# Written order on TensorE, hand-placed transposes of the norms, and raw weight sums by DMA, in a two-layer hybrid trunk

## The chip, the cores and the metric

The kernel runs on one core of a Trainium2 chip. The metric is device time in microseconds. Before the change three runs took 1724.76 us in the median (1724.73 to 1726.11). Engines: TensorE (PE in the profile, PEld its weight loads), VectorE (DVE), ScalarE (ACT), GpSimd (POOL) and SyncE (SP). SP issues plain loads, POOL issues the DMAs that add into what they write.

## What is computed

Two layers over 512 tokens of width 1024, all in float32:

```
x = x + 0.5 * SwiGLU_1(RMSNorm(x))          # width 2816
h = RMSNorm(x);  z = h @ W_in               # q, k, v, conv_B, conv_C, conv_h
x = x + concat([sliding-window attention, B * conv3(C * h_conv)]) @ W_out
x = x + 0.5 * SwiGLU_2(RMSNorm(x))
```

and a final RMSNorm. SwiGLU is `(silu(h @ w_gate) * (h @ w_up)) @ w_down`.

## The kernel before

**Products.** Every float32 operand is split in a high part (rounded to the format that TensorE takes, a ScalarE cast, L204) and a low part (the difference, a VectorE subtraction, L205): `hi`/`lo` for activations, `wh`/`wl` for weights. A product is three matmuls: high by high, low by high, high by low (`stream`, L781). Weights come in raw tiles of 128x1024 (tag `raw`, eight buffers); `wh` and `wl` have three buffers each, and `take_split` asks for a split two groups ahead of its use.

**Seven products for eight.** Most products are grouped in sevens (a Winograd form of Strassen's scheme). The weights' forms are a11, a12, s2, s3, s1, a22, s4, each in two halves h. Raw s1 and s3 are made on the way in: a load, and a second load that POOL's DMA adds to it (L199). Two more sums are made from raw tiles: a11 becomes s2 by adding s1 (L231), and a12 becomes s4 by adding a11 (L256 as a DMA, or L258 on VectorE), according to `how`. The activations' forms are b11, b21, t2, t3, t1, t4, b22 (`Seven.make`, L567 on); t2, for instance, is two VectorE sums (L578, L580), a cast and a subtraction. A form named in `far` is split otherwise (`split_far`, L207): ScalarE writes the negated source into the low part (L209), casts the high part (L210), and a POOL DMA adds the source to the low part (L211).

**Stages.** A SwiGLU is a list of stages: `w` takes two column blocks of gate and up at once (`winograd2`), with seven steps named by `CHAINS`: step 0 accumulates x from b11, step 1 w from b21, step 2 x again from t2, step 3 y from t3, then t1, t4, b22. Each step is 24 wide matmuls, two halves h by two token tiles u by six. `s` is the product with w_down shared in the same manner (`share`; x_s, y_s, w_s in the profile), `d` a plain down product (`down`, L309). The first SwiGLU has its own list (`FIRST`); the three others (`INNER`, `LAST`) begin with `w` on block 0 right after a norm. `mix` does the combined projection, attention and convolution, and multiplies by W_out with `share` in an early order of its own (x_m, y_m, w_m, z_m; `CHAINS_EARLY`), so that the first half of the tokens ends before the second. There t4 is the operand of step 4 (y_m), and t1, t4 and b22 are `far`.

**Norms.** A `Norm` is called with each finished tile of x. It adds the tile's squares (ScalarE). When the four pieces of a half of the tokens are there, `stage` (L522) computes the factor and, for each width half o and token tile t, scales (VectorE, `xn`, L546) and transposes (`turn`: four 128x128 transposes, L551, and copies, L554 to L557). For a norm ahead of a SwiGLU it then makes b11, b21 (after the first half) and t2 (after the second). The transposes take PSUM banks by tag: `aux`, `aux`, `sc`, `sc`, then `mm`, `mm`, `sc`, `sc` (ahead of a SwiGLU). The accumulators x take `mm` too, of which there are four.

**What sets the order.** Each engine issues in an order fixed when the program is made. The start is written by hand; all else is ordered by a scheduler that goes by the order of the code where it can, and on each engine takes a later instruction first when it expects the earlier one's inputs or buffers to be late. So PE's order before the change is nearly the written one, apart from transposes and a few products that were put back. In attention (`attend`) each step writes the product with the values, then the transposes of the probabilities (`Unit.turn`, L1285), then the next unit's scores (L1248, L1249).

Of the kernel before, what the change touches and what calls it, by code (L numbers as in the profile page):

```python
# [13 lines left out]
ALU = mybir.AluOpType  # L14

P = 128
# [56 lines left out]
def trunk_kernel(  # L73
# [53 lines left out]
    def small(name, n=NT, dt=F32):  # L127
        return work.tile([P, n], dt, tag="small", bufs=16, name=name)
# [84 lines left out]
    def need_split(g):  # L213
        while state["split"] <= min(g, len(order) - 1):
            n = state["split"]
            u, what = order[n]
            far = what == "far"
            if what in (None, "wide", "far"):
                need_raw(u if far else u + LOAD_AHEAD)
                raw = raw_of.pop(u)  # L220
            elif isinstance(what, tuple):

                what, h, how = what
                far = how == "far"
                last = {"a11": 0, "a12": 4, "s2": 2, "s3": 6, "s1": 2, "a22": 8, "s4": 4}[what]
                need_raw(u + h if far else u + max(last, 4) + h + LOAD_AHEAD)
                a11, s1, a12, s3, a22 = (raw_of.get(u + 2 * i + h) for i in range(5))
                if what == "s2":
                    late = state["late"] if h else None
                    with tc.issue_after(late) if late else nullcontext():  # L230
                        nc.vector.tensor_add(a11, a11, s1)  # L231
                raw = {"a11": a11, "a12": a12, "s2": a11, "s3": s3, "s1": s1, "a22": a22, "s4": a12}[what]
            else:

                need_raw(u + 4 + LOAD_AHEAD)
                a11, a12, s1, s3, a22 = (raw_of.get(u + i) for i in range(5))
                if what == "s2":
                    nc.vector.tensor_add(a11, a11, s1)
                if what == "s4":
                    nc.vector.tensor_add(a11, a11, a12)  # L240
                raw = {"a11": a11, "a12": a12, "s2": a11, "s3": s3, "s1": s1, "a22": a22, "s4": a11}[what]
                if what == FORMS[-1]:
                    for i in range(5):
                        del raw_of[u + i]
            shape = list(raw.shape)
            hi = wpool.tile(shape, F32R, tag="wh", bufs=3, name=f"wh_{n}")
            lo = wpool.tile(shape, F32R, tag="wl", bufs=3, name=f"wl_{n}")
            if far:
                sent = split_far(hi, lo, raw)
            else:  # L250
                split(hi, lo, raw)
            if isinstance(order[n][1], tuple):
                early = how == "early"
                if what == "s2" if early else what == "s3":
                    if how:
                        nc.gpsimd.dma_start(out=a12, in_=a11, accum_op=ALU.add)  # L256
                    else:
                        nc.vector.tensor_add(a12, a12, a11)  # L258
                done = {
                    "s2": (0,) if early else (),  # L260
                    "s3": (3,) if early else (0, 3),
                    "s1": (1,),
                    "a22": (4,),
                    "s4": (2,),
                }.get(what, ())
                for i in done:
                    del raw_of[u + 2 * i + h]
            split_of[n] = (hi, lo)
            state["split"] += 1
            if far:  # L270

                with tc.issue_after(sent.ins):
                    need_raw(u + LOAD_AHEAD + (4 + h if isinstance(order[n][1], tuple) else 0))
# [23 lines left out]
                nc.tensor.matmul(acc, lo[:, k, :], rhs[k][0], start=False, stop=k == last)  # L297
        return acc

    def down(acts, blocks):  # L300

        last = len(blocks) - 1

        def products(acc, t, i, wh, wl):
            tok = slice(t * P, (t + 1) * P)
            ah, al = acts[blocks[i]]
            for k in range(2):
                for n, (a, w) in enumerate(((ah, wh), (al, wh), (ah, wl))):
                    nc.tensor.matmul(  # L309
                        acc,  # L310
                        a[:, k, tok],
                        w[:, k, :],
                        start=i + k + n == 0,
                        stop=i == last and k == 1 and n == 2,
                    )

        for o in range(2):
            accs = [psum("mm", [P, S], f"down_{state['group']}_{t}") for t in range(NT)]
            if o and last:
                held = [take_split(SPLIT_AHEAD - i)[1:] for i in range(last + 1)]  # L320
                ahead = state["group"]
                for t in range(2):
                    for i, w in enumerate(held):
                        products(accs[t], t, i, *w)
                    yield t, o, accs[t]
                for i, w in enumerate(held):
                    for t in range(2, NT):
                        products(accs[t], t, i, *w)
                        if i == last:
                            yield t, o, accs[t]  # L330
                    need_split(ahead + i)
                continue
            for i in range(last + 1):
                _, wh, wl = take_split()
                for t in range(NT):
                    products(accs[t], t, i, wh, wl)
                    if i == last:
                        yield t, o, accs[t]

    def plan():  # L340
# [25 lines left out]
        def ffn(wg, wu, wd, stages):  # L366
            for what, b in stages:
# [3 lines left out]
                    up(wg, wu, b)  # L371
                if what == "w":
                    seven(
                        lambda o, j, h: ((wg, wu)[o], KC // 2 * j + 2 * h, 2, 2 * b * P, S), None
                    )
                if what == "s":
                    seven(
# [28 lines left out]
    def xt(t, o):  # L406
        return stream_of[2 * o + t // 2][:, t % 2, :]
# [60 lines left out]
    class Norm:  # L468
# [53 lines left out]
        def stage(self, half):  # L522

            i = self.i
            if half == 0:
                self.rooms()
            v, r, y = (small(f"{n}_{i}_{half}", 2) for n in "vry")
            at = 2 * half
            nc.vector.tensor_add(v, self.ss[:, at : at + 2], self.ss[:, NT + at : NT + at + 2])
# [1 line left out]
            nc.vector.tensor_scalar(v, v, 1.0 / D, EPS, op0=ALU.mult, op1=ALU.add)  # L531
            newton(y, r, v)
            for o in range(2):
                for t in (at, at + 1):
                    self.turn(t, o, y[:, t - at : t - at + 1])
                if half == 0 and not self.mixing:
                    self.make(("b11", "b21")[o])
            if half and not self.mixing:
                self.make("t2")

        def turn(self, t, o, by):

            name = f"{self.i}_{t}_{o}"
            tok = slice(t * P, (t + 1) * P)
            xn = g2(f"xn_{name}")
            nc.vector.scalar_tensor_tensor(  # L546
                xn, xt(t, o), by, self.gain[o], op0=ALU.mult, op1=ALU.mult
            )
            tp = psum(self.tags.pop(0), [P, KC // 2, P], f"xt_{name}")
            for j in range(KC // 2):  # L550
                nc.tensor.transpose(tp[:, j, :], xn[:, j * P : (j + 1) * P], ident)  # L551
# [220 lines left out]
                bias[:, h, :], df, -(2.0 ** -(h + 1)), m0, op0=ALU.mult, op1=ALU.add  # L772
            )

    def stream(accs, wh, wl, xh, xl, h, start):

        for u in range(2):
            tok = slice(u * P, (u + 1) * P)
            for k in range(2):
                for i, (x_, w) in enumerate(((xh, wh), (xl, wh), (xh, wl))):  # L780
# [5 lines left out]
                        stop=h + k == 2 and i == 2,  # L786
                        skip_group_check=not start,
                    )

    def share(ops, by, between=None, soon=None, after=None):  # L790

# [3 lines left out]
        for step, (acc, operand, start) in enumerate(chains):  # L795
# [4 lines left out]
                accs[acc] = [psum(tag, [P, S], f"{acc}_{ops.name}_{m}") for m in range(2)]  # L800
            for h in range(2):
                _, wh, wl = take_split()
                stream(accs[acc], wh, wl, xh, xl, h, start)
                if soon:
                    ops.make(*soon.get((step, h), ()))
                if h == 0:
# [18 lines left out]
    def ffn(norm, stages, whole, after=None, late=None):  # L825
# [100 lines left out]
        def winograd2(b, between=None):  # L926


            name = f"{whole}_{b}"
            accs = {}  # L930
            gates = [g2(f"gate_{name}_{t}") for t in range(NT)]
            ups = [None] * NT
            kept = {}
# [5 lines left out]
            for step, (acc, operand, start) in enumerate(CHAINS):  # L939
# [4 lines left out]
                    accs[acc] = [psum(tag, [P, S], f"{acc}_{name}_{u}") for u in range(2)]  # L944
                for h in range(2):
                    _, wh, wl = take_split()
                    stream(accs[acc], wh, wl, xh, xl, h, start)
                    for u in range(2):
                        out = accs[acc][u]
                        if h == 0:  # L950
# [18 lines left out]
                            nc.scalar.activation(gates[2 + u], out, AF.Silu)  # L969
                            nc.vector.tensor_mul(ups[2 + u], ups[2 + u], gates[2 + u])  # L970
                turns(step)
                if not first and step < 4:
                    norm.make(("t3", "t1", "t4", "b22")[step])
                if between:
                    between(step)
            if b in blocks:
# [38 lines left out]
        for i, (what, b) in enumerate(stages):  # L1015
# [25 lines left out]
            if final and not after:  # L1041
# [1 line left out]
                    [(acts[k][0][:, j, :], acts[k][1][:, j, :]) for k in b for j in range(2)]  # L1043
                )
                return
            for n, (t, o, acc) in enumerate(down(acts, b)):
                if b == (0,):
                    norm.make(*{0: ("t3",), 4: ("t1",)}.get(n, ()))
                nc.vector.scalar_tensor_tensor(
# [127 lines left out]
    def mix(l, norm, after):  # L1177
        q = [None] * NH

        mixed = [g8(f"m_{l}_{j}", F32, (P, KC // 2, S)) for j in range(2)]  # L1180
        ops = Seven(mixed, room_g8, f"m_{l}", far=("t1", "t4", "b22"))

        first = state["group"]
        held = [take_split(SPLIT_AHEAD - j) for j in range(3)]
# [1 line left out]
        for t in range(2):  # L1186
            tok = slice(t * H, (t + 1) * H)
            for j, (_, hi, lo) in enumerate(held):
                for k in range(KC):
                    xh, xl = (z[:, tok] for z in norm.h[k])  # L1190
                    for i, (w, x_) in enumerate(((hi, xh), (hi, xl), (lo, xh))):
# [5 lines left out]
                            stop=k == KC - 1 and i == 2,  # L1197
                            skip_group_check=True,
                        )
                if t:  # L1200
                    need_split(first + j + 3)

# [182 lines left out]
        late = ("sc", "sc", "aux", "aux") if mixing else ("mm", "mm", "sc", "sc")  # L1385
        return Norm(i, gain, mixing, ("aux", "aux", "sc", "sc") + late)

    for l in range(DEPTH):
        n1, n2 = stages_of(3 * l + 1), stages_of(3 * l + 2)
        n3 = stages_of(3 * l + 3) if l + 1 < DEPTH else None  # L1390
        ffn(norm, INNER if l else FIRST, 2 * l, n1, None if l else make_bias)
        mix(l, n1, n2)
        ffn(n2, INNER if n3 else LAST, 2 * l + 1, n3)
        norm = n3


# [28 lines left out]
```

## Time and profile before

| | us |
|---|---|
| median of three runs (lowest, highest) | 1724.76 (1724.73, 1726.11) |
| the profiled execution's own time | 1727.49 |
| its span, first to last instruction | 1725.7 |
| PE busy | 1685.2 (98%) |
| DVE busy | 1345.7 (78%) |
| ACT busy | 959.5 (56%) |
| POOL busy | 191.8 (11%) |
| mean granted TensorE clock | 0.992 |

Lines of a view are quoted as they stand. In a timeline a row is start, duration, engine, line, operation, output<-inputs by the program's names without numbers, shapes, and how many instructions were merged; in brackets the idle time before it and who ended it. A row of waits is who waited for whom, total, times and longest. A row of the table of stretches is the stretch, its length, and busy time with instructions of each engine, the granted clock, the DMA engines' busy share and GB/s. A row of a group ends with its total busy time and the mean ns of one, then the idle time before. Durations of matmuls overlap, since they are pipelined; what one costs is the distance from start to start.

### The profile page before, as it was taken

What the parts mean: (1) busy time and instruction counts of PE and PEld (TensorE: products, weight loads), DVE (VectorE), ACT (ScalarE), POOL (GpSimd) and SP (SyncE); (2) the same over time, 40 slices, a digit from 0 to 9 for tenths busy, and PEclk for the clock granted to TensorE, in tenths of its full rate; (3) what the DMA queues carried; (4) which work ended last, traced back from release to release, by engine and by line L of the source; (5) the groups of instructions that cost most, each with busy time, mean ns of one, the idle gap of its engine ahead of it and who ended that gap; (6) DMA issues with size and microseconds to landing.
All of it is one profiled execution on the core that took longest, in us unless ns stands there. A gap on an engine that the chain in (4) does not pass through costs nothing.

```text
span 1725.7 us, 21836 instructions
## 1 busy us (share of the span) xinstructions
PE 1685.2 (98%) x8150; PEld 1405.2 (81%) x8150; DVE 1345.7 (78%) x1762; ACT 959.5 (56%) x1369; POOL 191.8 (11%) x172
## 2 busy tenths in 40 slices
PE   9999999999988999999999999999999799999998
PEld 7888898898867888887778888878888678888877
DVE  7986689868779777799597776995578797776994
ACT  6545555556565555564455555644565655556553
POOL 0011111000210111011101111110002101111101
PEclk9999999999999999999999999999999989999999
DMA  8467788622694767678547776783127947767781
GB/s 244 103 180 194 183 205 210 166 66 62 153 225 123 207 172 189 179 191 222 147 122 196 186 180 184 191 219 112 39 74 166 212 133 191 188 171 190 189 207 49
DMA packets 188206, 285.62 MB, mean 166 GB/s; under 512 B 9124, under 2 KB 72132, under 8 KB 188100
## 3 DMA queue, kind: packets, MB, share of 16 engines
q1 hardware_dynamic: 146340, 204.91, 37.6%
q0 software_dynamic: 41056, 78.65, 26.9%
q8 instruction: 64, 1.05, 0.2%
q10 hardware_dynamic: 704, 0.66, 0.1%
q14 instruction: 42, 0.34, 0.1%
HBM read 268.46 MB, written 2.10 MB: 157 GB/s over the span
## 4 chain that ended last, share of the span: by engine, by line
PE 59%; DVE 6%; issue 2%; ACT 1%; DMA 1%; POOL 0%; ACTq 0%; POOLq 0%; DVEq 0%
PE x L781 18%; PE y L781 9%; PE x_s L781 6%; PE w L781 4%; PE y_s L781 4%; PE down L309 3%; PE x L896 2%; PE acc L291 2%; PE acc L292 2%; PE acc L294 2%; PE at L982 2%; DVE wl L205 1%; PE y L896 1%; DVE raw L231 1%; PE acc L1192 1%
## 5 line engine op out<-in xcount | busy, mean ns | idle before, releaser
L204 ACT CAST wh<-raw 128x1024 fp32r<-128x1024 f32 (+1 forms) x503 | 524.4, 1045 | 557.4 <-PE x L781 137.6
L205 DVE TENSOR_TENSOR wl<-raw,wh 128x1024 fp32r<-128x1024 f32 (+1 forms) x503 | 606.6, 1213 | 269.1 <-ACT wh L204 267.5
L781 PE MATMUL x<-wh,ft 128*128 128x512 f32 x608 | 189.6, 392 | 1.0 <-DVE ft L205 1.0
L781 PE MATMUL x<-wh,fb 128*128 128x512 f32 x608 | 188.5, 390 | 0.0
L781 PE MATMUL y<-wh,ft 128*128 128x512 f32 x608 | 188.5, 391 | 0.0
L781 PEld LDWEIGHTS x<-wh,ft 128*128 128x128 f32 x608 | 113.1, 188 | 25.1 <-DVE ft L205 2.2
L781 PEld LDWEIGHTS x<-wh,fb 128*128 128x128 f32 x608 | 114.3, 188 | 23.4
L781 PEld LDWEIGHTS y<-wh,ft 128*128 128x128 f32 x608 | 113.1, 188 | 22.7
L781 PE MATMUL x<-wl,fb 128*128 128x512 f32 x304 | 118.6, 390 | 0.0
L781 PE MATMUL x<-wl,ft 128*128 128x512 f32 x304 | 118.4, 390 | 0.0
L781 PE MATMUL y<-wl,ft 128*128 128x512 f32 x304 | 118.3, 389 | 0.0
L199 POOL DMA_DIRECT2D raw<-in_ffn_wu_dram x42 | 51.1, 1217 | 585.6 <-DMA raw<-in_ffn_wu_dram 405.2
L781 PE MATMUL w<-wh,fb 128*128 128x512 f32 x304 | 98.6, 409 | 5.3 <-ACT wh L204 5.3
L291 PE MATMUL acc<-hh,wh 128*128 128x512 f32 x240 | 94.6, 394 | 0.0
L294 PE MATMUL acc<-hh,wl 128*128 128x512 f32 x240 | 93.9, 391 | 0.0
L292 PE MATMUL acc<-hl,wh 128*128 128x512 f32 x240 | 93.6, 390 | 0.0
L309 PE MATMUL down<-wh,a 128*128 128x512 f32 x288 | 90.0, 392 | 0.0
L781 PE MATMUL y_s<-wh,ft_s 128*128 128x512 f32 x256 | 80.5, 392 | 5.4 <-ACT wh L204 5.4
L781 PE MATMUL x_s<-wh,ft_s 128*128 128x512 f32 x256 | 78.1, 393 | 1.2 <-ACT wh L204 1.0
L199 POOL DMA_DIRECT2D raw<-in_ffn_wg_dram x42 | 50.9, 1219 | 244.6 <-DVE wl L205 92.3
L781 PE MATMUL x_s<-wh,fb_s 128*128 128x512 f32 x240 | 74.0, 389 | 0.0
L781 PEld LDWEIGHTS w<-wh,fb 128*128 128x128 f32 x304 | 57.4, 195 | 19.6 <-ACT wh L204 8.2
(313 smaller groups left out, 3451.3 us busy)
## 6 DMA issues: line engine op xcount, KB each, us to landing
raw<-in_ffn_wu_dram SPq DMA_DIRECT2D x129, 512.0 KB, 3.7
raw<-in_ffn_wd_dram SPq DMA_DIRECT2D x104, 512.0 KB, 5.4
raw<-in_ffn_wg_dram SPq DMA_DIRECT2D x86, 512.0 KB, 5.0
raw<-in_ffn_wu_dram POOLq DMA_DIRECT2D x42, 512.0 KB, 7.7
raw<-in_ffn_wg_dram POOLq DMA_DIRECT2D x42, 512.0 KB, 6.3
raw<-in_w_in_dram SPq DMA_DIRECT2D x36, 512.0 KB, 3.8
raw<-in_ffn_wd_dram POOLq DMA_DIRECT2D x32, 512.0 KB, 7.8
raw<-raw POOLq DMA_DIRECT2D x20, 512.0 KB, 6.4
```

What stands on the lines that cost most here:

```text
L199: nc.gpsimd.dma_start(out=r, in_=rows_of(*more), accum_op=ALU.add)
L204: nc.scalar.copy(hi, raw)
L205: eng.tensor_sub(lo, raw, f32(hi))
L231: nc.vector.tensor_add(a11, a11, s1)
L291: nc.tensor.matmul(acc, hi[:, k, :], rhs[k][0], start=k == first, stop=False)
L292: nc.tensor.matmul(acc, hi[:, k, :], rhs[k][1], start=False, stop=False)
L294: nc.tensor.matmul(acc, lo[:, k, :], rhs[k][0], start=False, stop=k == last)
L309: nc.tensor.matmul(acc, a[:, k, tok], w[:, k, :], start=i + k + n == 0, stop=i == last and k == 1 and n == 2,)
L781: nc.tensor.matmul(accs[u], x_[:, 2 * h + k, tok], w[:, k, :], start=start and h + k + i == 0, stop=h + k == 2 and i == 2, skip_group_chec ...
L896: nc.tensor.matmul(out, w[:, k, cols], x_[:, k, :], start=start and k + i == 0, stop=k == KC // 2 - 1 and i == 2, skip_group_check=not start,)
L982: nc.tensor.transpose(tp[:, t * P : (t + 1) * P], ups[t][:, c * P : (c + 1) * P], ident)
L1192: nc.tensor.matmul(opened[j][:, tok], w[:, k, :], x_, start=t + k + i == 0, stop=k == KC - 1 and i == 2, skip_group_check=True,)
```

## The change

1. The whole loop over the layers runs under a manual schedule for PE: TensorE issues its instructions in written order. The other engines are ordered as before.
2. `Norm.stage` only scales; it puts the scaled tiles on a list, two at a time. `pull` takes one entry off, transposes it, and makes the forms that follow. `pull` is called at places written by hand: after the last product of token tiles 2 and 3 in `down` (L309); within the last step of `share` where a norm follows; within step 1 of the first `winograd2` pair after a norm; and twice in the opening groups of `mix` (L1192).
3. In the first pair after a norm t3 is made after step 1, t1 and t4 after step 2, b22 after step 3: one step later than before for t3, t1; t2 with the last pull.
4. The first pair of each `INNER` or `LAST` list has `how` = "light": a11 becomes s2 by a DMA on POOL that adds s1, written behind a11's split, and a12 becomes s4 by a DMA too. Two L231 adds and two L258 adds of each of the three pairs leave VectorE, and four 512 KB DMAs come for them.
5. In `mix`, t4 is no longer in `far`: its low part is a VectorE subtraction.

```diff
-                if what == "s2":
+                if what == "s2" and how != "light":
                     late = state["late"] if h else None
                     with tc.issue_after(late) if late else nullcontext():
                         nc.vector.tensor_add(a11, a11, s1)
...
+                if what == "a11" and how == "light":
+                    nc.gpsimd.dma_start(out=a11, in_=s1, accum_op=ALU.add)
                 if what == "s2" if early else what == "s3":
                     if how:
                         nc.gpsimd.dma_start(out=a12, in_=a11, accum_op=ALU.add)
...
                         if i == last:
                             yield t, o, accs[t]
+                            if norm:
+                                norm.pull()
...
-                        lambda o, j, h: ((wg, wu)[o], KC // 2 * j + 2 * h, 2, 2 * b * P, S), None
+                        lambda o, j, h: ((wg, wu)[o], KC // 2 * j + 2 * h, 2, 2 * b * P, S),
+                        "light" if b == 0 else None,
...
             for o in range(2):
+                xns = []
                 for t in (at, at + 1):
-                    self.turn(t, o, y[:, t - at : t - at + 1])
-                if half == 0 and not self.mixing:
-                    self.make(("b11", "b21")[o])
-            if half and not self.mixing:
+                    xns.append(g2(f"xn_{i}_{t}_{o}"))
+                    nc.vector.scalar_tensor_tensor(
+                        xns[-1],
+                        xt(t, o),
+                        y[:, t - at : t - at + 1],
+                        self.gain[o],
+                        op0=ALU.mult,
+                        op1=ALU.mult,
+                    )
+                self.waiting.append((half, o, xns))
+
+        def pull(self):
+
+            if not self.waiting:
+                return
+            half, o, xns = self.waiting.pop(0)
+            for t, xn in enumerate(xns):
+                self.turn(2 * half + t, o, xn)
+            if self.mixing:
+                return
+            if half == 0:
+                self.make(("b11", "b21")[o])
+            elif o:
                 self.make("t2")
...
     def stream(accs, wh, wl, xh, xl, h, start, norm=None):
...
+            if norm:
+                norm.pull()
...
-                stream(accs[acc], wh, wl, xh, xl, h, start)
+                stream(accs[acc], wh, wl, xh, xl, h, start, after if step == 6 else None)
...
-                    stream(accs[acc], wh, wl, xh, xl, h, start)
+                    stream(accs[acc], wh, wl, xh, xl, h, start, norm if fresh and step == 1 else None)
...
-                if not first and step < 4:
-                    norm.make(("t3", "t1", "t4", "b22")[step])
+                if fresh:
+                    norm.make(*{1: ("t3",), 2: ("t1", "t4"), 3: ("b22",)}.get(step, ()))
...
-            for n, (t, o, acc) in enumerate(down(acts, b)):
+            for n, (t, o, acc) in enumerate(down(acts, b, after if final else None)):
...
-        ops = Seven(mixed, room_g8, f"m_{l}", far=("t1", "t4", "b22"))
+        ops = Seven(mixed, room_g8, f"m_{l}", far=("t1", "b22"))
...
+                    if t == 0 and (j, k) in ((1, KC - 1), (2, KC // 2 - 1)):
+                        norm.pull()
...
-    for l in range(DEPTH):
+    with tc.manual_schedule(engines={pe}):
+        for l in range(DEPTH):
```

More of the change, by code (lines that the diff above doesn't have):

```diff
@@ L298, in group, with down @@
         return acc
-    def down(acts, blocks):
+    def down(acts, blocks, norm=None):
         last = len(blocks) - 1
@@ L526, in stage @@
                 self.rooms()
+                self.waiting = []
             v, r, y = (small(f"{n}_{i}_{half}", 2) for n in "vry")
@@ L533, in stage, with turn @@
             for o in range(2):
+                xns = []
                 for t in (at, at + 1):
-                    self.turn(t, o, y[:, t - at : t - at + 1])
-                if half == 0 and not self.mixing:
-                    self.make(("b11", "b21")[o])
-            if half and not self.mixing:
+                    xns.append(g2(f"xn_{i}_{t}_{o}"))
[19 more added lines that the diff above has]
+            elif o:
                 self.make("t2")
-        def turn(self, t, o, by):
+        def turn(self, t, o, xn):
             name = f"{self.i}_{t}_{o}"
             tok = slice(t * P, (t + 1) * P)
[L545 to L548, printed above, removed]
             tp = psum(self.tags.pop(0), [P, KC // 2, P], f"xt_{name}")
@@ L773, in make_bias, with stream @@
             )
-    def stream(accs, wh, wl, xh, xl, h, start):
+    def stream(accs, wh, wl, xh, xl, h, start, norm=None):
         for u in range(2):
@@ L930, in winograd2 @@
             accs = {}
+            fresh = b == 0
             gates = [g2(f"gate_{name}_{t}") for t in range(NT)]
@@ L1386, in stages_of @@
         return Norm(i, gain, mixing, ("aux", "aux", "sc", "sc") + late)
-    for l in range(DEPTH):
[L1389 to L1394, printed above, removed]
+    with tc.manual_schedule(engines={pe}):
+        for l in range(DEPTH):
+            n1, n2 = stages_of(3 * l + 1), stages_of(3 * l + 2)
+            n3 = stages_of(3 * l + 3) if l + 1 < DEPTH else None
+            ffn(norm, INNER if l else FIRST, 2 * l, n1, None if l else make_bias)
+            mix(l, n1, n2)
+            ffn(n2, INNER if n3 else LAST, 2 * l + 1, n3)
+            norm = n3
 _INS = [
```

## The prediction

> **What bounds the kernel now.** I read the page first, for the engine that has least room:
>
> ```profile
> PE 1685.2 (98%) x8150; PEld 1405.2 (81%) x8150; DVE 1345.7 (78%) x1762; ACT 959.5 (56%) x1369; POOL 191.8 (11%) x172
> ```
>
> TensorE (PE) is the bound nearly everywhere, so a change can win only what PE waits, or runs slowly, now. The waits of PE say for whom, in total, times and longest:
>
> ```profile
> PE y_m L781 <- DMA ft_m<-sums_m: 9.5, 2, 4.9
> PE w L781 <- DVE wl L205: 7.2, 4, 2.7
> PE y_s L781 <- ACT wh L204: 5.4, 6, 0.9
> PE w L781 <- ACT wh L204: 5.3, 6, 0.9
> PE x_m L781 <- DVE wl L205: 1.7, 2, 0.9
> ```
>
> Three places: y_m in the output product of each mixing layer; w, the second product of the first gate/up pair after a norm; and y_s in the shared down products. A table of stretches shows what they cost, the granted clock (PEclk) included. First two rows: the y_m wait of layer 0; third: norm to third product, layer 0; fourth: steady state; the 862 rows: the norm between the layers; the last three: layer 1's y_m and norm.
>
> ```profile
> core 0: us, PE busy (x) PEld busy (x) DVE busy (x) ACT busy (x) POOL busy (x), PEclk, DMA share, GB/s
> 491.60:496.40 4.80, 0.25 (x2) 0.00 (x0) 3.39 (x4) 0.93 (x1) 0.00 (x0) 0.86 1.04 294
> 496.40:502.00 5.60, 5.53 (x13) 4.38 (x14) 0.00 (x0) 0.85 (x1) 2.42 (x2) 0.51 0.74 234
> 518.40:538.70 20.30, 15.87 (x67) 11.89 (x67) 19.41 (x27) 8.47 (x15) 0.00 (x0) 0.92 0.17 30
> 560.00:720.00 160.00, 160.00 (x739) 132.79 (x738) 111.43 (x113) 88.34 (x113) 19.44 (x16) 1.00 0.74 187
> 862.50:870.00 7.50, 4.77 (x17) 2.73 (x17) 7.50 (x13) 2.77 (x7) 0.00 (x0) 1.00 0.00 0
> 870.00:874.00 4.00, 4.00 (x16) 3.26 (x17) 3.69 (x5) 1.18 (x2) 0.00 (x0) 0.57 0.00 0
> 862.50:881.50 19.00, 16.15 (x66) 11.83 (x66) 17.96 (x24) 7.82 (x14) 0.00 (x0) 0.91 0.05 10
> 1350.00:1355.00 5.00, 0.13 (x1) 0.00 (x0) 3.27 (x4) 0.92 (x1) 0.00 (x0) 1.00 1.04 298
> 1355.00:1359.00 4.00, 3.96 (x10) 3.12 (x11) 0.00 (x0) 0.00 (x0) 0.88 (x1) 0.57 0.71 271
> 1376.00:1397.70 21.70, 17.91 (x67) 13.52 (x67) 19.61 (x26) 8.02 (x15) 0.00 (x0) 0.76 0.19 35
> ```
>
> In steady state PE never idles and DVE has 30% to spare (111 of 160). After a norm DVE is the full one (19.41 of 20.30), and PE waits for its low parts (wl). After the long y_m waits the clock is at about half.
>
> For unit costs I take two pieces of PE's time, 24 wide products in 5.44 us and four transposes between two products (874.08 to 874.75, less one product):
>
> ```profile
> 543.91 5.44 PE y L781 x24
> ```
>
> ```profile
> 874.08 0.48 PE L781 MATMUL x<-wh,fb 128*128 128x512 f32 x1
> 874.39 0.60 PE L551 MATMUL xt<-ident,xn 128*128 128x128 f32 x4
> 874.75 0.48 PE L781 MATMUL x<-wl,fb 128*128 128x512 f32 x1
> ```
>
> So a wide product is 0.227 us and a transpose 0.11 us.
>
> **The change, part by part.** The sum is made against the profiled execution (1727.5 us, span 1725.7); the median of the runs shown is 1724.8, 2.7 lower, and the difference found is taken off that.
>
> *t4 out of the far forms.* The low part of form t4 of the mixing output came by a DMA; it is now one DVE subtraction. The DMA rows (KB, median us to landing; the first is a plain load):
>
> ```profile
> raw<-in_ffn_wu_dram SPq DMA_DIRECT2D x129, 512.0 KB, 3.7
> ...
> raw<-raw POOLq DMA_DIRECT2D x20, 512.0 KB, 6.4
> ...
> ft_m<-sums_m POOLq DMA_DIRECT2D x2, 512.0 KB, 9.6
> ```
>
> Gone per layer: two ScalarE passes for one cast, one 512 KB DMA on POOL's queue, and the wait behind it. Layer 0: 4.80-0.25 = 4.55 us idle and 5.60 us at clock 0.51, so 2.74 lost; layer 1: 4.87 and 4.00 x 0.43 = 1.72. Together 13.9 us. Late next is DVE: the subtraction (1.22 us, as L231 below) falls ahead of the wl split for which x_m already waits 0.9 us. Hidden it costs 0, wholly on the path 2.4 for both; I take 1.8, nearer the latter since x_m waits. Gain 12.1. Loads that the wait let catch up (294 GB/s there) could be late next; the steady state moves 187 GB/s and makes PE wait for none, so I count nothing.
>
> *The norm's transposes by hand, and the first pair's order.* In the trace w, written second, runs ahead of x, because x waits for accumulators that the second half's transposes were given. The weight splits come in written order with three buffers, so w waits at each. In written order x goes first with splits that stand ready. The three stretches (20.3, 21.7, 19.0 us) hold some 50 wide products and 16 transposes, 50 x 0.227 + 16 x 0.11 = 13.1 us: lost are 7.2, 8.6 and 5.9, together 21.7.
>
> What takes the place? The second half's last transposes stand after the first quarter-and-half of step 1 (w), with 12 products, 2.7 us, and two more that need only the high part, before form t2's low part is needed. What t2 needs, on DVE, with ScalarE's cast between (before the last row):
>
> ```profile
> 531.85 1.28 DVE L557 COPY hf<-xt 128x512 f32<-128x512 f32 x2
> 533.23 1.22 DVE L578 TENSOR_TENSOR sums<-hf,hf 128x1024 f32<-128x1024 f32 x1
> 534.49 1.22 DVE L580 TENSOR_TENSOR sums<-sums,hf 128x1024 f32<-128x1024 f32 x1
> 535.63 1.22 DVE L205 TENSOR_TENSOR wl<-raw,wh 128x1024 fp32r<-128x1024 f32 x1
> 536.76 0.68 DVE L955 TENSOR_TENSOR gate<-w,p 128x512 f32<-128x512 f32 x1
> 537.37 2.35 DVE L205 TENSOR_TENSOR ft<-sums,ft 128x1024 fp32r<-128x1024 f32 x2
> ```
>
> From 531.85 to the end of the first ft, 538.59: 6.7 us with a wl and a gate between; a cast is about the 1.2 us that these fill, so 5.6 to 6.7 after the copies can start. Less 2.7 and part of the first copy PE now waits 2.6 to 4.0 us at step 2, with all its later products queued behind; I take 3.0. At the first hand-placed transposes another 0.5 (0 to 1) in the two norms after mixing. In the norm between the layers step 0 starts on form b11, whose two copies, cast and subtraction (1.28 + 1.2 + 1.22 = 3.7 us by the same rows) have 6 products and 8 transposes (2.2 us) as cover, with the square of the last tile in ScalarE's queue as well: 1.6 (1.2 to 2.0). A slow clock after: 0.7 each, between 0 and the 1.7 of 870 to 874. That leaves 4.2, 4.2 and 5.3, so 21.7-13.7 = 8.0 gained. In the two mixing norms the transposes stand where PE ran them already or a step later, covered by the six to 36 products behind: nothing, at worst 1 each.
>
> [...]
>
> *Raw sums by DMA.* Per inner first pair two L231 and two L258 adds leave DVE:
>
> ```profile
> L231 DVE TENSOR_TENSOR raw<-raw,raw 128x1024 f32<-128x1024 f32 x58 | 70.3, 1220 | 0.5
> ```
>
> At 1.22 us each 12 adds are 14.6 us of DVE, 4.9 per stretch that is full: this is what lets the t2 chain above run nearly undisturbed, and has no gain of its own. It adds 12 DMAs on POOL's queue, each waiting for a split and a load; queued behind are the next accumulating loads. Landing 6.4 to 9.6 us later, a11's sum is needed four groups, 10.9 us of PE, after its split: hidden; it comes into the open only beyond that.
>
> *Written order elsewhere.* In the mixing layers the probabilities' transposes (pt) are written ahead of the next unit's scores (sc); PE ran them behind:
>
> ```profile
> 388.96 0.28 PE L1248 MATMUL sc<-k,q 128*128 128x256 f32 x1
> ...
> 390.38 0.33 PE L1285 MATMUL pt<-ident,p 128*128 128x128 f32 x1
> ...
> 404.59 0.28 PE L1248 MATMUL sc<-k,q 128*128 128x256 f32 x1
> ...
> 406.70 1.02 PE L1285 MATMUL pt<-ident,p 128*128 128x128 f32 x7
> ```
>
> ```profile
> 389.63 0.48 DVE L1252 CUSTOM_DVE_ANT_0 p<-sc,bias,sink 128x256 f32<-128x256 f32 x1
> ...
> 390.04 0.87 DVE L1277 TENSOR_SCALAR p<-p,sums 128x128 f32<-128x128 f32 x4
> ```
>
> In written order PE stands at 388.96 until p is there. If p comes no sooner that is 1.4 and 2.1 us, and I put the unit between at half the first, 0.7: 4.2 a layer. But DVE scaled p (L1277) behind work on the very scores (L1252) that now come later, so I take half, 2.1 a layer, 4.2 in all (0 to 8.4); what queues behind is the next scores. In the shared products PE filled its wait for wl with two high products of x_s and two of y_s:
>
> ```profile
> 758.34 1.19 PE L781 MATMUL x_s<-wh,ft_s 128*128 128x512 f32 x4
> 760.43 0.73 PE L781 MATMUL y_s<-wh,ft_s 128*128 128x512 f32 x2 [0.90 <-ACT wh L204]
> ```
>
> ```profile
> 759.33 2.36 DVE L205 TENSOR_TENSOR wl<-raw,wh 128x1024 fp32r<-128x1024 f32 x2
> ```
>
> In written order the third product waits for the first wl (about 760.5) with two done, where PE had done four by 760.43 and six by 761.01: 0.4 lost, six times, 2.4 (0 to 5.4, four products each).
>
> Sum: 12.1 + 8.0 - 4.2 - 2.4 = 13.5 us. 1727.5 - 13.5 = 1714.0 profiled, 1724.8 - 13.5 = **1711.3** as median.
>
> **The rivals.** *The stalls only change place.* The norm stretches keep their 21.7 us, since t2 is as late as w was. For it: DVE is full there. Against: 4.9 us of DVE work leave each. 12.1 - 6.6 = 5.5 gained: 1719.3; with attention at its upper bound 1723.5.
>
> *Slower: a buffer that comes free late.* a11's raw buffer was free after two DVE adds; it now waits for two DMAs in turn, and the next load takes its place. 2 x 6.4 to land, 3.7 for the load and 2.4 for a split (two passes of 1.2) are 18.9 us, against five steps, 29 us of PE with the transposes, from its split to step 5, which needs a22. It decides from (29 - 6.1)/2 = 11.5 us a DMA, not far above the 9.6 of the busy stretch; at 15 us each it costs 7 us in three pairs, 21 against 13.5, some 8 slower: 1733. For it: POOL's queue is in order and its DMA waits are long; against: DMA share is 0.17 and 0.05 in two of the three stretches. [...]
>
> *More than forecast.* t2 hidden, clock untouched, p in time: 12.1 + 15 - 4 = 23: 1702.
>
> *Order is no change.* If PE's order had been the written one already, only t4 and the adds remain; the pt, y_s and w rows above exclude it.
>
> **How the numbers follow.** Forecast 60% (1706 to 1716), stalls moved 20%, more gain 10%, slower 10%. Leaving out the slow case and the far ends, 1702 to 1723 holds eight in ten. A measurement here tells about 0.2%, 3.4 us. Faster by more: 60 + 10 + 13 = 83%; within: the upper part of stalls moved, 7%; slower: 10%.
>
> **What would show it.** No y_m wait for a DMA and clock 1.00 behind it (else t4 is wrong); x ahead of w after each norm and a wait of x for ft at step 2 near 3 us; pt waits of one to two us in attention; x_s for wl instead of y_s for wh. A PE wait for wh or wl in step 2 or 5 of a first pair, released by a raw DMA, would prove the slower rival.

## The result and the profile after

The changed kernel takes 1743.65 us (1742.49 to 1744.54), the kernel before 1725.43 beside it: ratio 1.0104 (95% interval 1.0086 to 1.0121), some 18 us **slower**. The forecast was 1711.3 in 1702 to 1723. The profiled execution has a span of 1741.8 us, 16.1 more than before. First the page's line of engines, then PE's waits:

```profile
PE 1684.2 (97%) x8150; PEld 1408.8 (81%) x8150; DVE 1336.0 (77%) x1752; ACT 957.0 (55%) x1367; POOL 200.8 (12%) x182
```

```profile
PE xt L573 <- DVE xn L543: 14.9, 3, 7.8
PE x L803 <- ACT ft L204: 11.4, 3, 3.8
PE x_s L803 <- DVE wl L205: 8.1, 6, 1.5
PE x L803 <- DVE ft L205: 4.5, 3, 1.6
PE pt L1312 <- DVE p L1304: 3.7, 6, 0.9
PE x_m L803 <- DVE wl L205: 2.5, 2, 1.2
...
PE at L1007 <- DVE p L995: 1.1, 1, 1.1
PE x L803 <- DVE fb L205: 0.8, 1, 0.8
...
PE x L803 <- ACT fb L204: 0.4, 1, 0.4
```

PE has the same work, and DVE 9.7 us less. The y_m wait for a DMA is gone, and so are the waits of w. In their place stand 14.9 us of transposes (xt) waiting for scaled tiles (xn), and 15.9 us of step 2 (x) waiting for form t2 (ft). The table of stretches, of after: the old y_m place and the stretch behind it, twice (rows 1, 2 and 5); rows 3 and 6 run from the end of z_m to the first product of step 3 (y); row 4 is the steady state:

```profile
core 0: us, PE busy (x) PEld busy (x) DVE busy (x) ACT busy (x) POOL busy (x), PEclk, DMA share, GB/s
491.00:496.00 5.00, 4.91 (x21) 4.05 (x22) 4.94 (x7) 4.05 (x7) 0.00 (x0) 1.00 1.10 216
496.00:502.00 6.00, 6.00 (x28) 4.97 (x27) 5.21 (x7) 2.46 (x3) 1.19 (x1) 1.00 0.93 300
514.34:551.55 37.21, 24.12 (x90) 19.11 (x88) 25.55 (x33) 17.87 (x25) 5.98 (x6) 0.77 0.60 128
560.00:720.00 160.00, 160.00 (x739) 132.77 (x738) 111.19 (x112) 88.38 (x113) 19.71 (x17) 1.00 0.73 185
...
1346.00:1351.00 5.00, 5.00 (x24) 4.14 (x23) 5.00 (x6) 3.10 (x4) 1.52 (x2) 1.00 1.19 203
1382.55:1418.60 36.05, 23.99 (x90) 18.93 (x88) 25.42 (x33) 17.80 (x25) 5.26 (x6) 0.76 0.62 132
```

The same stretch, z_m to y, of before:

```profile
517.43:543.75 26.32, 21.09 (x89) 16.07 (x89) 25.43 (x33) 14.47 (x23) 0.00 (x0) 0.94 0.26 60
1375.09:1402.78 27.69, 23.15 (x89) 17.73 (x89) 25.48 (x32) 13.98 (x22) 0.00 (x0) 0.82 0.26 57
```

The y_m stretches are full at clock 1.00, as forecast; the steady state is the same. The two norms after mixing became 10.9 and 8.4 us longer with the same products, idle and slow (layer 0: 13.1 us without a product, 5.2 before; 24.1 us busy, 21.1 before). Why, ScalarE's timeline of after shows (layer 0; z_m ends at 514.34):

```profile
519.18 0.18 ACT L511 ACTIVATION_READ_ACCUMULATOR sq<-x 128x1 f32 x1
525.40 1.04 ACT L204 CAST wh<-raw 128x1024 fp32r<-128x1024 f32 x1 [6.04 <-DMA raw<-raw]
526.36 0.29 ACT L536 ACTIVATE r<-v,eps 128x2 f32<-128x2 f32 x1
```

The norm's root (r) needs the last squares, done at 519.4. It starts 7 us later, because a weight cast stands ahead of it in ScalarE's queue, and this cast waits for a DMA. That DMA is the new raw sum, second row of POOL's timeline (L255 is a11 += s1):

```profile
514.62 2.44 POOL L199 DMA_DIRECT2D raw<-in_ffn_wg_dram  x2 [11.01 <-DVE hf L579]
516.52 2.37 POOL L255 DMA_DIRECT2D raw<-raw  x2
```

Issued behind two accumulating loads, it lets the cast start 8.9 us later. Step 2, which needs this weight, starts only at 541.79; the norm behind it in the queue was in a hurry. VectorE has the same: its subtraction wl waits for the cast and stands ahead of Newton's steps and xn.

```profile
526.48 1.23 DVE L205 TENSOR_TENSOR wl<-raw,wh 128x1024 fp32r<-128x1024 f32 x1 [5.59 <-ACT wh L204]
...
528.27 2.74 DVE L543 SCALAR_TENSOR_TENSOR xn<-x,y,gain 128x512 f32<-128x512 f32 x4
```

On PE, in written order, the transposes wait for xn with everything behind them, and later step 2 waits for t2's cast and then for its subtraction:

```profile
529.08 1.97 PE L573 MATMUL xt<-ident,xn 128*128 128x128 f32 x8 [7.78 <-DVE xn L543]
533.41 1.83 PE L573 MATMUL xt<-ident,xn 128*128 128x128 f32 x8
541.79 0.76 PE L803 MATMUL x<-wh,ft 128*128 128x512 f32 x1 [3.83 <-ACT ft L204]
544.03 0.79 PE L803 MATMUL x<-wh,ft 128*128 128x512 f32 x1 [1.47 <-DVE ft L205]
```

### The profile page after: what moved, and what is told of

The parts are those of the page before. It is cut to its first block, busy times and chain, and to the rows that moved or that the text cites. A ratio compares the mean times of both kernels' runs of the same rounds, so it can differ in the third digit from the quotient of the medians.

```text
span 1741.8 us, 21884 instructions
## 1 busy us (share of the span) xinstructions
PE 1684.2 (97%) x8150; PEld 1408.8 (81%) x8150; DVE 1336.0 (77%) x1752; ACT 957.0 (55%) x1367; POOL 200.8 (12%) x182
## 4 chain that ended last, share of the span: by engine, by line
PE 85%; DVE 10%; DMA 2%; issue 2%; ACT 1%; POOL 0%; SPq 0%; ACTq 0%; DVEq 0%; POOLq 0%
PE x L803 23%; PE y L803 12%; PE x_s L803 7%; PE down L311 6%; PE w L803 5%; PE y_s L803 5%; PE acc L293 3%; PE acc L294 3%; PE acc L296 3%; DVE wl L205 3%; PE x L920 3%; PE at L1007 2%; PE acc L1217 2%; PE y L920 1%; PE x_m L803 1%
## 5 line engine op out<-in xcount | busy, mean ns | idle before, releaser
L803 PE MATMUL x<-wh,ft 128*128 128x512 f32 x608 | 195.2, 402 | 16.0 <-ACT ft L204 11.4
L803 PEld LDWEIGHTS x<-wh,ft 128*128 128x128 f32 x608 | 116.2, 193 | 42.5 <-ACT ft L204 12.7
L803 PEld LDWEIGHTS x<-wl,ft 128*128 128x128 f32 x304 | 58.7, 193 | 12.4
```

The source lines that it names most:

```text
L803: nc.tensor.matmul(accs[u], x_[:, 2 * h + k, tok], w[:, k, :], start=start and h + k + i == 0, stop=h + k == 2 and i == 2, skip_group_chec ...
```

## The experiments

First theory: written order takes away PE's freedom to do other products while the norm's chain is late, and the sums by DMA only feed this. Rival: the DMAs themselves are what is late. Four kernels each make or undo one part.

**t4_alone**, the kernel before with

```diff
-far=("t1", "t4", "b22")
+far=("t1", "b22")
```

> The kernel before with only t4 taken out of the far forms. If my first term holds (13.9 us of wait and slow clock less about 1 us of longer x_m wait, as the trace after shows), 12 to 13 us faster than before: about 1712. If the removed wait comes back elsewhere (weights that arrive late after mixing), 0 to 6 us faster.

Measured: 1711.23 us, ratio 0.992 (0.9905 to 0.9935), 13.5 below before. The y_m wait is gone, and the step for t4 (12.1) holds. x_m waits 1.5 us here, no longer than before (1.7).

**light_alone**, the kernel before with the raw sums by DMA (part 4) and nothing else.

> The kernel before with only the raw sums of the first pair by DMA; TensorE's order stays with the scheduler and t4 stays far. Theory (the loss needs the DMA and the written order together): here ScalarE has the norm factor ahead of the cast of s2, so nothing of the norm waits for the DMA; with 4.9 us of VectorE work less in each full stretch it is 0 to 6 us faster than before. Rival (the DMA is late by itself): PE waits for the split of s2 at step 2 and it is 5 us or more slower than before.

Measured: 1717.57 us, ratio 0.9957 (0.9943 to 0.9972), 7.2 below before, a little more than the 0 to 6 expected. Here the scheduler keeps the root ahead of the cast, and the first xn is done 6.8 us behind z_m (which ends at 517.4), against 11.4 before:

```profile
523.48 2.74 DVE L549 SCALAR_TENSOR_TENSOR xn<-x,y,gain 128x512 f32<-128x512 f32 x4
```

**no_light**, the changed kernel without part 4:

```diff
-                        "light" if b == 0 else None,
+                        None,
```

> The kernel after with the raw sums of the first pair made by VectorE again; written order, hand-placed transposes and t4 stay. Theory: after the change ScalarE's queue holds the cast of s2 ahead of the second half's norm factor, and that cast waits for the light DMA, so the transposes wait 7.8 and 6.8 us; without the DMA the cast does not wait, PE's wait for xn falls below 2 us each, and the time falls by 12 to 17 us, to 1727 to 1732. Rival (the hand placement itself is too early, the DMAs are innocent and relieve VectorE): the transposes still wait 5 us or more each and the time stays at 1740 or above.

Measured: 1737.73 us, ratio 1.0073 (1.0056 to 1.0090). Taking the DMAs away returns 6 us, where 12 to 17 were expected, and leaves the kernel 13 us above before.

```profile
PE x L803 <- ACT ft L204: 11.4, 3, 3.8
PE xt L573 <- DVE xn L543: 8.3, 3, 4.0
```

Without them xn is still 4 us late, because now VectorE's two L231 adds stand ahead of it. The trace of **before** had shown it, on DVE between z_m's end (517.43) and xn:

```profile
522.39 1.22 DVE L231 TENSOR_TENSOR raw<-raw,raw 128x1024 f32<-128x1024 f32 x1
...
523.67 1.22 DVE L231 TENSOR_TENSOR raw<-raw,raw 128x1024 f32<-128x1024 f32 x1
...
524.87 1.22 DVE L258 TENSOR_TENSOR raw<-raw,raw 128x1024 f32<-128x1024 f32 x1
...
526.92 1.23 DVE L205 TENSOR_TENSOR wl<-raw,wh 128x1024 fp32r<-128x1024 f32 x1 [0.77 <-ACT wh L204]
528.07 2.73 DVE L546 SCALAR_TENSOR_TENSOR xn<-x,y,gain 128x512 f32<-128x512 f32 x4
```

**order_alone**, the changed kernel without parts 4 and 5.

> The kernel after without the light DMAs and with t4 far again: written order and hand placement alone. Theory: the t2 waits of about 6 us in three norms, attention (2.3 a layer) and the shared products (about 1.4 in all) stand against what the w waits cost before (21.7): within 6 us of before on the slow side, 1725 to 1735, and 12 to 13 above no_light. Rival (hand placement is the whole loss): 1750 or above.

Measured: 1747.03 us, ratio 1.0133 (1.0115 to 1.0151), 22 above before, with the same 8.3 us of xn waits. Neither side had this: 1725 to 1735 was expected, 1750 or more by the rival. Written order with the new places costs this much by itself; parts 4 and 5 aren't needed for the loss.

Second theory: two causes, who stands ahead of the norm's chain on ScalarE and VectorE, and that PE may not pass a late product. Four kernels.

**t4_light**, the kernel before with parts 4 and 5, PE's order the scheduler's.

> The kernel before with two of the changes: t4 out of the far forms, and the raw sums by accumulating DMA; TensorE's order stays the scheduler's, the norm's transposes stay where they were. Theory (each change works on its own stretch: t4 on the output products of the mixing layers, 13.5 us; the sums on the norm stretches, 7.2 us): the two add up, about 1704 us, 20 below before, and the whole slowdown of the changed kernel lies in the order. Rival (both draw on the same slack of VectorE and of the DMA queue of GpSimd, or the sums' gain needs the DMA that t4 gives up): 1709 or more.

Measured: **1705.41 us** (1702.95 to 1706.29), ratio 0.9886 (0.9871 to 0.9901). The gains add (13.5 + 7.2 = 20.7 expected, 19.4 found). It beats both kernels. Its longest waits, and its two stretches from z_m to y:

```profile
PE w L784 <- DVE wl L205: 6.5, 3, 2.7
```

```profile
509.45:534.42 24.97, 21.32 (x89) 17.25 (x89) 23.10 (x30) 14.57 (x22) 5.18 (x6) 0.86 0.83 169
1355.28:1380.57 25.29, 21.62 (x89) 17.50 (x89) 23.09 (x30) 14.57 (x22) 4.93 (x6) 0.87 0.84 167
```

**no_manual**, the changed kernel with

```diff
-    with tc.manual_schedule(engines={pe}):
+    with nullcontext():
```

> The changed kernel with the manual schedule of TensorE taken away: the transposes and forms are still written at their new places, the scheduler orders TensorE. Theory A (what costs is that TensorE may not go past a product whose operand is late): most of the loss returns, 1704 to 1715 us, and the waits of xt for xn at the first norm fall under 2 us. Theory B (what costs is that the norm's operations are written later, so that the weight cast of step 2 stands ahead of the norm's root in ScalarE's queue; this kernel's ScalarE order has it so too): the xn waits of 7 to 8 us stay or come out as waits of other products at the same place, and the time is 1725 us or more.

Measured: 1724.34 us, ratio 0.9998 (0.9989 to 1.0008): 19 us come back, as theory A had it, but the time is 9 us above A's range and within 0.7 of B's, and the xn waits stay, as B had it. The root stands behind the cast here too:

```profile
PE xt L573 <- DVE xn L543: 11.3, 2, 6.8
PE x L803 <- ACT ft L204: 8.1, 2, 4.3
```

**after_r_first**, the changed kernel, the cast and subtraction of s2 issued behind the norm's root and last xn (`state["norm"]`):

```diff
+            elif isinstance(order[n][1], tuple) and what == "s2" and how == "light":
+                with ExitStack() as behind:
+                    for ins in state["norm"]:
+                        behind.enter_context(tc.issue_after(ins))
+                    split(hi, lo, raw)
...
```

> The changed kernel, but the weight cast and subtraction of step 2 of each first pair (whose raw tile is the sum that arrives by DMA) are issued behind the norm's root on ScalarE and the last xn on VectorE. Theory (the root stood in ScalarE's queue behind a cast that waited for a DMA): the xn waits of 7.8 and 6.8 us fall below 1.5 each, two norms, and the time is 1728 to 1733 us (12 us of waits less what the later weight cast gives back at the products of step 2). Rival (the waits come from the DMA's lateness itself, and move to the products that need this weight): 1738 us or more.

Measured: 1732.54 us, ratio 1.0044 (1.0027 to 1.0061), 11 us faster than the changed kernel. The cast still waits 4.5 us for its DMA (6.0 in the changed kernel); what changed is who stands behind it.

```profile
PE x L809 <- ACT ft L204: 15.7, 3, 6.8
...
PE x L809 <- DVE ft L205: 5.9, 3, 2.1
...
PE xt L579 <- DVE xn L548: 2.2, 3, 1.0
```

The xn waits fall by 12.7 us, but 5.7 us come back at t2, whose copies now queue behind the cast.

**t2_first**, in addition the gates of step 1 and the later forms issued behind t2's cast and subtraction:

```diff
-                            nc.vector.tensor_add(gates[u], out, kept["p1", u])
-                            nc.scalar.activation(gates[u], gates[u], AF.Silu)
+                            with behind(*norm.seven.t2) if fresh else nullcontext():
                                 nc.vector.tensor_add(gates[u], out, kept["p1", u])
                                 nc.scalar.activation(gates[u], gates[u], AF.Silu)
...
-                if fresh:
+                with behind(*norm.seven.t2) if fresh and step else nullcontext():
                   if fresh:
```

> As the last one, and in addition the gates of step 1 and the forms that follow t2 are issued behind t2's cast and subtraction on ScalarE and VectorE. Theory (t2's cast waits behind a table load and a gate on ScalarE, and its subtraction behind two adds of VectorE): the waits of x for ft at step 2, about 6 us in each of three norms, fall to 3 or 4, and the time is 5 to 8 us below that of the last kernel. Rival (those operations stand in the gap of the chain and delay nothing, or what they feed is late next): within 3 us of it.

Measured: 1726.09 us, ratio 1.0008 (0.9998 to 1.0017), 6.5 below the last one. In the changed kernel a table load and a gate stood ahead of t2's cast:

```profile
538.88 1.28 ACT L981 ACT_TABLE_LOAD   x1
540.17 0.63 ACT L981 ACTIVATE gate<-gate 128x512 f32<-128x512 f32 x1
540.71 1.03 ACT L204 CAST ft<-sums 128x1024 fp32r<-128x1024 f32 x1
```

The gain is inside the forecast of 5 to 8, but not where that put it: the waits for t2's cast fell from 15.7 to 12.8 only, those for its subtraction from 5.9 to 1.4.

```profile
PE x L816 <- ACT ft L204: 12.8, 3, 5.0
...
PE x L816 <- DVE ft L204: 1.4, 3, 0.5
```

Last, whether the two causes add, and what the places and the attention cost by themselves.

**r_first_free** and **t2_free**, after_r_first and t2_first without the manual schedule.

> The kernel with the root alone ahead (1732.5 us), and the manual schedule taken away. Theory of two causes that add: 1724.3 - 11.2 = 1713 us, 1710 to 1716. Rival (a free TensorE covers the late root as w's products cover the late xn in the kernel before): 1720 us or more, near the 1724.3 of the kernel with a free order alone.

> The kernel with root and t2 ahead on ScalarE and VectorE (1726.1 us), and the manual schedule of TensorE taken away. Theory (two causes that add: who stands ahead of the norm's chain on ScalarE and VectorE, 17.6 us; that TensorE may not pass a late product, 19.4 us as found without the mended chain): 1704 to 1710 us, as fast as the kernel with t4 and the sums alone (1705.4). Rival (with the chain mended there is little left for a free TensorE to go round, so the two overlap): 1715 us or more.

Measured: 1720.57 us (0.9974, 0.9963 to 0.9985) and 1716.42 us (0.9945, 0.9930 to 0.9960). My theory of two causes that simply add falls: with PE free the same mends win 3.8 and 7.9 us, not 11.1 and 17.6. They overlap, as both rivals had it, and 11 us to t4_light remain.

**mix_written**, t4_light with PE in written order in the mixing layers ahead of W_out.

> The kernel with t4 and the sums alone (1705.4 us), TensorE in written order from the first product of each mixing layer to the last product ahead of W_out, nowhere else. Theory (the changed kernel's three pt waits of a layer, 2.35 us, are the whole cost there): 1709 to 1711 us. Rival (the waits only take the place of others, or the clock and the next stage pay more): 1705 to 1707, or 1713 and more.

Measured: 1711.17 us, ratio 0.9916 (0.9900 to 0.9933), 5.8 above t4_light, at the upper edge of what was expected.

```profile
PE pt L1290 <- DVE p L1282: 3.7, 6, 0.9
```

**all_written**, t4_light under the manual schedule, the transposes at their old places.

> The kernel with t4 and the sums alone, TensorE in written order through all layers, with the norm's transposes where the kernel before writes them: all of a half's at once, ahead of step 0. Theory (the places by hand are worth something in written order, and it is the order that costs): each norm ahead of a SwiGLU then waits for xn0, 6.8 us, and for the copies behind, against about 8 us of waits of the kernel with root and t2 ahead; the mixing norms wait as well, some 5 to 9 us each, which hand placement spared them: 1735 to 1755 us. Rival (the hand placement is itself what costs): 1726 us or less.

Measured: 1765.20 us, ratio 1.0229 (1.0214 to 1.0244). Dearer than expected:

```profile
PE xt L554 <- DVE xn L549: 43.7, 11, 4.3
```

All with t4 and the sums as changed, median us:

| norm's code | PE written order | PE by the scheduler |
|---|---|---|
| old places | 1765.2 | **1705.4** |
| new places | 1743.7 (the change) | 1724.3 |
| new places, root ahead | 1732.5 | 1720.6 |
| new places, root and t2 ahead | 1726.1 | 1716.4 |

"New places" stands for parts 2 and 3 together; neither was run without the other. Placing by hand is worth 21.5 us where PE can't go round a late product, and costs 19 where it can. What it costs there after both mends, 11 us, I read from the traces only. In t4_light PE does 12 products of w, then the transposes, and has some 34 products behind them while t2 is made; its one long wait (2.7 us, for wl) falls early. In t2_first PE does 30 products, the transposes, and has 12 behind them. In layer 0 step 2 starts as late in both, 19.5 and 19.2 us behind z_m, since the chain from z_m through root, xn, transposes, sums and cast sets it. But in t2_first the wait (4.9 us) stands at the end of the chain, and the slow clock after it is paid in full: step 2 takes 8.8 us, in t4_light 5.4. This row of t2_first begins where step 2 does:

```profile
533.63:539.69 6.06, 5.59 (x12) 4.08 (x13) 5.81 (x7) 3.42 (x5) 0.00 (x0) 0.51 0.60 205
```

In t4_light the slow clock follows the early wait and lies where PE would have waited for the chain anyway: from 515.07 to 518.06 its seven products are 0.43 us apart, against 0.227 by the forecast's unit cost.

```profile
514.48 0.79 PE L784 MATMUL w<-wl,fb 128*128 128x512 f32 x1 [2.72 <-DVE wl L205]
515.07 1.05 PE L784 MATMUL w<-wh,fb 128*128 128x512 f32 x2
```

With PE free (t2_free) both count: step 2 starts 20.7 us behind z_m in layer 0 and takes 7.5, so that this stretch is 3.2 us longer than t4_light's:

```profile
508.47:536.67 28.20, 20.62 (x90) 15.95 (x88) 24.32 (x32) 16.78 (x24) 5.47 (x6) 0.88 0.79 168
```

In layer 1 it is 5.3 us longer (22.4 us to step 2, where t4_light has 19.9). A kernel that shifts only the pulls was not run.

## Why the prediction was wrong

**t4 out of far: right.** 12.1 forecast, 13.5 alone. The 1.8 that I allowed for the subtraction was not there: x_m waits 1.5 us in t4_alone. The 2.5 in the changed kernel come with the written order, since order_alone, with t4 still far, has 2.4. In that order t4 is worth less, 9.3 us (order_alone less no_light).

**The norms with transposes placed by hand: the step that failed.** I had 21.7 us lost before and 13.7 after. From z_m, or the last down product, to y lie 72 products and 16 transposes, 18.1 us by my unit costs. Before, the three stretches take 26.3, 27.7 and 25.1 us (861.57 to 886.70 between the layers), so 24.8 are lost. After, they take 37.2, 36.1 and 27.7 us (868.37 to 896.93, less 0.9 for eight transposes more), so 46.6 are lost, 21.8 more. Term by term, all three norms:

| us | forecast | changed kernel |
|---|---|---|
| transposes wait for xn | 1.0 | 14.9 |
| step 2 waits for t2 | 9.0 | 15.9 |
| x waits for b11 (fb) | 1.6 | 1.2 |
| slow clock | 2.1 | some 14.6 (an estimate: the rest) |
| sum | 13.7 | 46.6 |

"At the first hand-placed transposes another 0.5" became 7.8 us in layer 0 and 6.8 in layer 1. That 0.5 had no row under it. The adds ahead of xn were in the trace of before, and following xn there (first done 11.4 us behind z_m, against 30 products, 6.8 us) would have given 4.6, near the 4.0 that order_alone and no_light measure. With the root ahead it is 1.0, the upper end I had given: for this wait the place was not bad, the chain was late. The wait at t2, 3.0 a norm (2.6 to 4.0), was 3.8 for the cast; a second, 1.5 for the subtraction, was left out, since I let DVE run "nearly undisturbed" where gates and the next form's sum went ahead: from the first copy to the end of the first ft the chain took 9.5 us (534.50 to 543.97), not 5.6 to 6.7. The clock, 0.7 us a norm, costs some 6 us in each of the two after mixing, the 24 us that PE is busy there less 18.1 (an estimate).

**Raw sums by DMA: failed with it.** I called them "hidden", with "no gain of its own". With PE free they win 7.2 us, since VectorE's adds stood ahead of xn; with the change's order they cost about 6, so 24 of the 30 us missed in the norms are there without them. I named who was queued behind the new DMAs on POOL, but not who was queued behind their *consumer*: the cast of s2 on ScalarE, with the norm's root behind it. Issuing that cast later alone returned 11 us, and then the sums win 5 in the written order too (1732.5 against the 1737.7 of no_light).

**Attention: right in kind, small in size.** Forecast 4.2 (0 to 8.4), measured 5.8 (mix_written). The pt waits are 3.7 of it, at most 0.9 each where one to two us were to show; the rest is no more than t4_light's runs differ.

**Shared products: right.** x_s for wl stands in the place of y_s for wh, 8.1 for 5.4 us, so 2.7 against 2.4. Unforeseen: 1.1 us at L1007, in the first SwiGLU.

From these the norms and the sums together cost 18.2 + 13.5 - 5.8 - 2.7 - 1.1 = 22 us, as the stretches above say, where I had 8.0 as gain. **The slower rival** had 10%, the right sign and the right DMA, but the wrong victim: it wanted PE to wait for a late wh or wl in step 2 or 5, from 11.5 us a DMA on. At 8.9 us the weight itself was in time, and PE never waited for it. **Stalls change place** had the right picture, but no room for a chain that gets longer.

On the clock, the forecast's 0.7 us a norm was an estimate between 0 and the 1.7 us of 870 to 874 in before. After's stretch from the first wait of step 2 on:

```profile
541.79:551.55 9.76, 8.28 (x25) 6.28 (x25) 7.37 (x7) 5.22 (x7) 0.00 (x0) 0.65 0.18 54
```

The clock is 0.65 here, behind waits of 3.83 and 1.47 us, and 0.51 in t2_first behind one of 4.93. Shorter waits had slow products behind them as well: t4_light's 2.72 us, which follows one of 0.93, has them 0.43 us apart, against the 0.227 of the forecast's unit cost, and in the kernel before the 2.74 us behind layer 0's mixing are followed by a clock of 0.54 (522.46 to 526.00). So the forecast was right to count some slow clock behind the new waits, and still allowed too little.

## What to carry to other kernels

With PE's order fixed, a late operand became idle time of PE (14.9 us of waits for xn in the changed kernel), so before fixing an engine's order follow each chain that feeds it, on the other engines' queues and against the products that stand ahead. When an operation is replaced by a DMA, ask who is queued behind the instruction that reads the result: here ScalarE's cast waited 6.04 us for the new sum, and the norm's root behind it started 7 us after its last squares. And parts of a change should be tried alone; two of these five made the kernel 19 us faster, and with the other three it was 18 us slower than before.

## What the runs showed of the hardware

In layer 0 of the changed kernel a 512 KB add from one tile to another, issued behind two accumulating loads, let its reader start 8.9 us after issue. The median landing of this kind is 6.4 us there, with 32 of them, as in the kernel before with 20:

```profile
raw<-raw POOLq DMA_DIRECT2D x32, 512.0 KB, 6.4
```

In t4_light and t2_first, what a wait cost went with where its slow clock fell. t4_light's stretch in layer 0 (clock 0.86) is 3.0 us shorter than that of t2_first, whose mean clock is no lower (0.88). Both reach step 2 about equally late, but t4_light's slow products lie ahead of it:

```profile
514.44:542.43 27.99, 21.64 (x89) 16.72 (x88) 23.91 (x31) 16.18 (x23) 5.46 (x6) 0.88 0.79 169
```
